# Sums with ones for the inverse roots at the gate and in the last product, and two of that product's four tiles in full width

## The chip, the cores and the metric

The kernel runs on one core of a Trainium2 chip. The metric is the device time of one execution in microseconds (us); lower is better. The profile is one execution recorded by the hardware profiler; its times count from the start of its span. The engines are called PE (TensorE's matmuls; PEld is its weight loads), DVE (VectorE), ACT (ScalarE), POOL (GpSimd) and SP (SyncE, which issues most DMAs).

## The reference

One decoder layer on 2048 tokens of 1024 channels, in float32: an RMSNorm, an input projection, two groups of heads (a gated linear recurrence and a sliding-window attention), an output projection, a second RMSNorm, a gated MLP, and a last RMSNorm. What matters here is the end of it:

```python
def rmsnorm(x, w, eps=EPS):
    inv = lax.rsqrt(jnp.mean(x * x, axis=-1, keepdims=True) + eps)
    return x * inv * w

h = h + mix @ w_out
v = rmsnorm(h, norm_ffn_w)
gate = causal_depthwise_conv(v @ w_gate, conv_w, conv_b)
h = h + (jax.nn.silu(gate) * (v @ w_up)) @ w_down
return rmsnorm(h, final_norm_w)
```

D_MODEL is 1024, the width of the MLP 2816. Each rmsnorm needs, for every token, the inverse root of the mean of 1024 squares.

## The kernel before, in words

**Layout.** Channels lie on the 128 partitions, tokens along the free dimension. The tokens go through the layer in two passes of 1024 (`hf` 0 and 1). A pass has the mixer stage, `out_proj` (line 785), `gate_up` (line 981) and `down` (line 1066); the end of `down` in pass 0 already loads and projects pass 1.

**Numbers in two parts.** A float32 operand of a large product is split into two float32r parts, the rounded value (`hi`, a cast on ACT, line 758) and the rest (`lo`, a subtraction on DVE, line 759); three matmuls (hi by hi, hi by lo, lo by hi) make the product. A matmul whose operands are plain float32, as the ones below, is carried out in two passes, and the profile shows two matmuls for it.

**Seven products.** `gate_up` and `down` multiply two-by-two blocks with seven products in place of eight (Strassen and Winograd's scheme). In `down` the products are called P1, P5, P6, P3, P7, P2 and P4 (the order in which they run); each runs over 11 blocks of 128 rows of `w_down`, taken in six pieces (five of two blocks, one of one) that SP loads and ACT and DVE split (`prep_piece`, line 1104). A product makes four output tiles (`d` 0 to 3) of 128 channels by 512 tokens, each in a PSUM bank of its own (`pdx` or `pdy`); `product` (line 1143) issues the three matmuls of each block, lines 1151 to 1153. After P2 the tokens' first half (`lo`, 512 of the pass's 1024) lacks only P4 in its upper four channel tiles; the second half (`hi`) was complete after P7.

**Sums of squares.** An object of `Stats` (line 241) keeps in `acc` the sum over the channel tiles of the squares (ACT squares, line 253; DVE adds, line 256), so that 128 partial sums per token are left, one in each partition. There are two ways from there to the inverse root:

- `inverse` (line 267) and `spread` (line 310): for each 128 tokens a matmul of `acc` as weights with one column of ones (line 276) puts the sum of a token into its own partition, as one column; `rsqrt` (line 170) works on 128x2 or 128x4 elements (DVE, three Newton steps from an integer guess; or, with `table`, ACT's Sqrt, a reciprocal and one step); the result is laid on a diagonal with the identity (line 284), and a matmul with ones (line 316) brings it to all partitions. In the last use, a series of 7 matmuls without use keeps PE at work meanwhile (`without_use`, line 281, `TAIL_WARM`).
- `everywhere` (line 296): a matmul of a 128x128 matrix of ones with `acc` (line 302) gives every partition the full sum of each token at once; ACT takes an approximate inverse root (line 304, `Abs_reciprocal_sqrt`) and its square (line 306), and DVE makes one Newton step at full width (lines 305, 307, 308). Its scratch tiles come from the ring `ut` of seven 128x512 tiles.

**At the gate.** In the first pair of channel tiles of `gate_up`, `everywhere` runs ahead of the product S4 (line 1012) over the pass's 1024 tokens, in two sums of 512. The roots scale the gate's tiles (line 1003) and later products; DVE and ACT split the next operands in the same stretch.

**P4 in the last pass.** The loop of `down` is left before P4 (line 1179), and P4 is written out (lines 1210 to 1234). The 512 tokens are taken in two halves of 256: for each half, for each of the four tiles, all 33 matmuls of 256 columns, then the addition to the residual (`add`, line 1137), its square and its sum (`st.add`), and the scaling by the final weight (`weigh`, line 1134). `inverse`, `spread` and `finish` of the 512 tokens that were complete before (`s2`) stand behind tiles of the first half, and those of the first 256 behind tiles of the second half. At the end come those of the last 256; there the square of the last tile isn't added to `acc` but summed by matmuls of its own. ACT loads its table for Sqrt ahead of that (line 1221).

**`finish`** (line 1241) multiplies the eight channel tiles by the root (line 1244, DVE) and issues a store after each (line 1245), on SP, or on ACT and SP in turn for the last 256.

**The order of the work.** The program text sets priorities; when the kernel is built, a scheduler with a timing model puts the instructions of each engine in a fixed order, by priority among those that it takes to be ready. `tc.issue_after(x)` puts what is traced within behind `x` on x's engine. Each engine then works in that order and waits on semaphores.

Of the kernel before, what the change touches and what calls it, by code (L numbers as in the profile page):

```python
# [8 lines left out]
F32 = mybir.dt.float32  # L9
F32R = mybir.dt.float32r  # L10
# [7 lines left out]
P = 128  # L18
# [22 lines left out]
UT = 7  # L41
# [12 lines left out]
def hymba_layer(ctx: ExitStack, tc: tile.TileContext, a: dict, out: bass.AP):  # L54
# [9 lines left out]
    wp = pool("w")  # L64
    hp = pool("h")
    sp = pool("small", bufs=2)
    sp.tile([P, 16], F32, name="pad", bufs=1)
    dp = pool("dram", space=bass.MemoryType.DRAM)
    mmp = pool("mm", bufs=4, space=PSUM)
    hgp = pool("hgp", bufs=2, space=PSUM)  # L70
# [3 lines left out]
    def ps(kind, name):  # L74
        return spaces[kind].tile([P, 512], F32, tag=kind, name=name)
# [164 lines left out]
    class Stats:  # L240
# [52 lines left out]
            nc.sync.dma_start(row, self.acc[0:1])  # L293
            nc.sync.dma_start(rs, row.rearrange("o (c t) -> (o t) c", t=P))

        def everywhere(self, part, kinds):

            n = self.acc.shape[-1]
            for b in range(n // 512):
                a = self.acc[:, b * 512:(b + 1) * 512]  # L300
                s = ps(kinds[b % 2], "psum")
                marks["psum"] = nc.tensor.matmul(s, ones, a, start=True, stop=True)
                y, t = part("y"), part("t")
                nc.scalar.activation(y, s, AF.Abs_reciprocal_sqrt, scale=1.0 / D, bias=eps)
                nc.vector.tensor_scalar(a, s, -0.5 / D, -0.5 * EPS, op0=ALU.mult, op1=ALU.add)
                nc.scalar.activation(t, y, AF.Square)
                nc.vector.tensor_tensor(t, t, a, op=ALU.mult)
                nc.vector.scalar_tensor_tensor(a, t, 1.5, y, op0=ALU.add, op1=ALU.mult)

        def spread(self, bank=None):  # L310

# [445 lines left out]
    def split_into(h, l, src, eng=None):  # L757
        return (nc.scalar.copy(h, src),  # L758
                (eng or nc.vector).tensor_tensor(l, src, h.bitcast(F32), op=ALU.subtract))  # L759
# [221 lines left out]
    def gate_up(hf, ops, hs, nxt, last, p):  # L981

        acts = {op: [dp.tile([P, n, 512], F32, name=f"act{hf}{op}{i}") for i, n in enumerate(PIECES)] for op in OPS}
        lo, hi = slice(0, 512), slice(512, HALF)
        invb = hs.acc

        def ring(name):
            return p.tile([P, 512], F32, tag="ut", name=name, bufs=UT)

        srcs = [w[2 * pr:2 * pr + 2] for pr in range(FT // 2) for w in (a["w_gate"], a["w_up"])]  # L990
        for pr in range(FT // 2):
            f0 = 2 * pr
            W, nxt = nxt, None

            ga = [p.tile([P, HALF + 64], F32, tag="ga", name="ga", bufs=2)[:, 0:2 + HALF] for _ in range(2)]

            def gate(i, j, x, y):
                dst = ga[i][:, 2 + j * 512:2 + (j + 1) * 512]
                iv = invb[:, j * 512:(j + 1) * 512]
                if y is not None:  # L1000
                    nc.vector.tensor_tensor(dst, x, y, op=ALU.add)
                    x = dst
                later.append(lambda: nc.vector.tensor_tensor(dst, x, iv, op=ALU.mult))
                if pr:
                    flush()

            def flush():
                while later:
                    later.pop(0)()

            later = []
            then = {"S4": lambda: hs.everywhere(ring, ("mm", "mm")), "A22": flush} if pr == 0 else {}
# [12 lines left out]
            for i in range(2):  # L1025
                ft, g = f0 + i, ga[i]
                nc.scalar.copy(g[:, 0:2], halo[:, ft])
# [36 lines left out]
        return acts  # L1064

    def down(hf, kept, acts, p):
# [4 lines left out]
        lo, hi = slice(0, 512), slice(512, HALF)  # L1071
        final = hf + 1 == NH
        NP = len(PIECES)
        def ring(name):
            return p.tile([P, 512], F32, tag="ut", name=name, bufs=UT)

        todo = [(name, w, t, j) for name, w, t in PRODUCTS for j in range(NP)]
        S = {}
# [53 lines left out]
        def weigh(d, bs):  # L1132
            t = hh[d][:, bs]
            return nc.scalar.activation(t, t, AF.Identity, scale=C.fnw[:, d:d + 1])

        def add(t, o):
            nc.vector.tensor_tensor(t, t, o, op=ALU.add)

        def done(st, d, bs):
            st.add(hh[d][:, bs])  # L1140
# [65 lines left out]
        if final:  # L1206
            for k in range(end + 3, len(todo)):
                ready[k] = prep_piece(k)

            steps = [(st, slice(i * 256, (i + 1) * 256)) for i, st in enumerate(s1.halves())]  # L1210
            for i, (st, bs) in enumerate(steps):
                for d in range(4):
                    for k in range(end, len(todo)):
                        product(k, bx[d][:, bs], d, bs)
                    t = hh[d + 4][:, bs]
                    add(t, bx[d][:, bs])
                    last = st.add(t, i == 1 and d == 3)
                    weighed = weigh(d + 4, bs)
                    if i and d == 0:
                        with tc.issue_after(weighed.ins):  # L1220
                            nc.scalar.activation(warm, ones[:, 0:1], AF.Sqrt)
                    if i == 0 and d == 0:
                        s2.inverse("o2")
                    elif i == 0 and d == 2:
                        s2.spread()
                        finish(hf, hh, s2, hi, [nc.sync])
                    elif i and d == 0:
                        steps[0][0].inverse("o")
                    elif i and d == 1:
                        inv = steps[0][0].spread(0)  # L1230
                    elif i and d == 2:
                        finish(hf, hh, steps[0][0], steps[0][1], [nc.sync], inv)
            steps[1][0].inverse("o", last)
            finish(hf, hh, steps[1][0], steps[1][1], [nc.scalar, nc.sync], steps[1][0].spread(1))
# [6 lines left out]
    def finish(hf, hh, st, bs, queues, inv=None):  # L1241
        for d in range(KT):
            t = hh[d][:, bs]
            nc.vector.tensor_tensor(t, t, st.acc if inv is None else inv, op=ALU.mult)
            queues[d % len(queues)].dma_start(out[d, :, hf * HALF + bs.start:hf * HALF + bs.stop], t)

    X = []
# [96 lines left out]
```

## Time and profile before

| what | us |
|---|---|
| median of 3 runs | 2122.56 |
| lowest and highest run | 2122.28 and 2124.97 |
| time of the profiled execution | 2122.11 |
| its span, first to last instruction | 2120.3 |

A line of the page's part 1 gives, per engine, the busy time, its share of the span and the number of instructions. A line of a timeline gives the start and the length (us), the engine, the line of the kernel, the operation, output and inputs by the program's names, the shapes, and in brackets the engine's idle time before it with the instruction that ended the wait. Rows named `x4` are merged from four instructions. A matmul's length runs from its start to the modelled end of its pipeline, so successive matmuls overlap; the distance between starts is the pace. A line of the chain of waits gives start, length, engine, output and line of one link.

### The profile page before, as it was taken

How to read it: one execution, taken by the hardware profiler on the slowest of the kernel's cores; microseconds unless marked ns; L12 is line 12 of the kernel's file. 1: busy time of each engine (PE TensorE's matmuls, PEld its weight loads, DVE VectorE, ACT ScalarE, POOL GpSimd, SP SyncE). 2: the span in 40 equal slices, each digit the busy share in tenths (PEclk: the TensorE clock that was granted, in tenths of full speed). 3: DMA queues.
4: the chain of work that ended last, by engine and by line, in shares of the span. 5: the costliest groups of instructions: out<-in, count | busy, mean ns of one | idle time of the engine just before them, and what ended most of it. 6: DMA issues, size and time to landing. Idle time of an engine off the chain costs nothing.

```text
span 2120.3 us, 29895 instructions
## 1 busy us (share of the span) xinstructions
PE 2108.2 (99%) x11584; PEld 1749.3 (83%) x11584; DVE 1624.7 (77%) x2374; ACT 1096.6 (52%) x1880; POOL 21.6 (1%) x52
## 2 busy tenths in 40 slices
PE   9999999999999999999999999999999999999998
PEld 7888888888888888888888888888888888888888
DVE  7457787898878878775863677868988787887766
ACT  6456675664444444435734476656544444443453
POOL 1000000000000000000000000000000000000000
PEclk9999999999999999999999999999999999999999
DMA  4111111423332325954731111213223223279643
GB/s 161 43 40 39 37 41 53 174 75 101 105 118 85 124 90 189 396 199 161 238 108 50 33 34 34 80 52 139 95 90 125 94 95 119 85 247 368 227 134 135
DMA packets 96475, 255.21 MB, mean 120 GB/s; under 512 B 17354, under 2 KB 19658, under 8 KB 96332
## 3 DMA queue, kind: packets, MB, share of 16 engines
q1 hardware_dynamic: 91076, 251.32, 34.6%
q10 hardware_dynamic: 5256, 1.98, 0.4%
q8 instruction: 91, 1.49, 0.3%
q14 instruction: 52, 0.43, 0.1%
HBM read 195.11 MB, written 57.16 MB: 119 GB/s over the span
## 4 chain that ended last, share of the span: by engine, by line
PE 82%; DVE 1%; DMA 1%; ACT 1%; issue 0%; DVEq 0%; ACTq 0%
PE pop L222 8%; PE X L933 7%; PE X L934 7%; PE X L935 7%; PE Y L933 4%; PE Y L934 4%; PE Y L935 4%; PE pdx L1151 3%; PE pdx L1153 3%; PE pdx L1152 3%; PE pdy L1151 3%; PE pdy L1153 3%; PE pdy L1152 3%; PE q L222 2%; PE g L222 2%; PE f L222 2%
## 5 line engine op out<-in xcount | busy, mean ns | idle before, releaser
L758 ACT CAST whi<-raw 128x1024 fp32r<-128x1024 f32 x88 | 92.7, 1053 | 102.9 <-PE X L934 61.1
L933 PE MATMUL X<-T,whi 128*128 128x512 f32 x352 | 137.0, 389 | 0.0
L934 PE MATMUL X<-T,whi 128*128 128x512 f32 x352 | 137.0, 389 | 0.0
L935 PE MATMUL X<-T,wlo 128*128 128x512 f32 x352 | 136.9, 389 | 0.0
L1032 DVE SCALAR_TENSOR_TENSOR y<-ga,cw,y 128x1024 f32<-128x1024 f32 x88 | 112.5, 1280 | 28.4 <-ACT y L1030 28.2
L940 ACT COPY u<-X 128x512 f32<-128x512 f32 x88 | 51.7, 587 | 124.1 <-PE X L935 124.1
L201 DVE TENSOR_TENSOR wlo<-raw,whi 128x1024 fp32r<-128x1024 f32 x57 | 69.4, 1222 | 59.4 <-ACT whi L200 59.0
L200 ACT CAST whi<-raw 128x1024 fp32r<-128x1024 f32 x57 | 59.4, 1048 | 95.7 <-PE hq L222 29.2
L759 DVE TENSOR_TENSOR wlo<-raw,whi 128x1024 fp32r<-128x1024 f32 x88 | 107.3, 1220 | 0.3 <-ACT whi L758 0.3
L222 PE MATMUL pop<-XH,whi 128*128 128x512 f32 x256 | 87.8, 393 | 0.0
L222 PE MATMUL pop<-XL,whi 128*128 128x512 f32 x256 | 87.4, 390 | 0.0
L222 PE MATMUL pop<-XH,wlo 128*128 128x512 f32 x256 | 87.0, 390 | 0.0
L759 DVE TENSOR_TENSOR xld<-raw,xhd 128x1024 fp32r<-128x1024 f32 x72 | 81.0, 1132 | 7.7 <-ACT xhd L758 7.5
L631 ACT COPY G<-QK 128x1024 f32<-128x1024 f32 x48 | 51.5, 1072 | 56.3 <-DVE QK L653 50.7
L758 ACT CAST xhd<-raw 128x1024 fp32r<-128x1024 f32 x72 | 69.5, 978 | 20.7 <-DMA raw<-act0B 5.8
L933 PEld LDWEIGHTS X<-T,whi 128*128 128x128 f32 x352 | 66.1, 188 | 14.1 <-ACT u L940 0.4
L934 PEld LDWEIGHTS X<-T,whi 128*128 128x128 f32 x352 | 66.1, 188 | 13.7
L935 PEld LDWEIGHTS X<-T,wlo 128*128 128x128 f32 x352 | 66.1, 188 | 13.7
L1151 PE MATMUL pdx<-xhd,hid 128*128 128x512 f32 x192 | 74.6, 392 | 0.9 <-ACT hid L758 0.6
L653 DVE TENSOR_TENSOR QK<-QK,f 128x1024 f32<-128x1024 f32 x56 | 68.5, 1223 | 8.3 <-ACT G L631 7.6
L1152 PE MATMUL pdx<-xld,hid 128*128 128x512 f32 x192 | 74.8, 389 | 0.0
L1153 PE MATMUL pdx<-xhd,lod 128*128 128x512 f32 x192 | 73.7, 389 | 0.0
(394 smaller groups left out, 6328.7 us busy)
## 6 DMA issues: line engine op xcount, KB each, us to landing
wr<-in_w_down SPq DMA_DIRECT2D x90, 512.0 KB, 4.7
raw<-in_w_gate SPq DMA_DIRECT2D x44, 512.0 KB, 3.6
raw<-in_w_up SPq DMA_DIRECT2D x44, 512.0 KB, 3.6
raw<-act0T SPq DMA_DIRECT2D x20, 512.0 KB, 5.5
raw<-act1T SPq DMA_DIRECT2D x20, 512.0 KB, 8.6
act0B<-y SPq DMA_DIRECT2D x33, 256.0 KB, 2.6
act1B<-y SPq DMA_DIRECT2D x33, 256.0 KB, 2.7
raw<-in_w_out SPq DMA_DIRECT2D x16, 512.0 KB, 5.6
```

Of the source, the lines that this page charges most:

```text
L201: nc.vector.tensor_tensor(lo, raw, hi.bitcast(F32), op=ALU.subtract)
L222: marks["unit"] = nc.tensor.matmul(o[b], w, x[:, bs], start=f, stop=l)
L653: done = nc.vector.tensor_tensor(own, own, Fv.rearrange("p b w -> p w b").unsqueeze(3).to_broadcast([P, 2, nb, m]), op=ALU.mult)
L758: return (nc.scalar.copy(h, src), (eng or nc.vector).tensor_tensor(l, src, h.bitcast(F32), op=ALU.subtract))
L759: (eng or nc.vector).tensor_tensor(l, src, h.bitcast(F32), op=ALU.subtract))
L933: nc.tensor.matmul(o, wh[:, ws], xh, start=i == 0 and not more, stop=False, skip_group_check=more)
L934: nc.tensor.matmul(o, wh[:, ws], xl, start=False, stop=False, skip_group_check=more)
L935: r = nc.tensor.matmul(o, wl[:, ws], xh, start=False, stop=i == 3, skip_group_check=more)
L1032: nc.vector.scalar_tensor_tensor(y, g[:, w:w + HALF], C.cw[:, ft, w:w + 1], y, op0=ALU.mult, op1=ALU.add)
L1151: nc.tensor.matmul(o, wh[:, i, c], ah[:, i, cols], start=f, stop=False, skip_group_check=more)
L1152: nc.tensor.matmul(o, wh[:, i, c], al[:, i, cols], start=False, stop=False, skip_group_check=more)
L1153: nc.tensor.matmul(o, wl[:, i, c], ah[:, i, cols], start=False, stop=l, skip_group_check=more)
```

## The change

Four edits.

1. `everywhere` can make its sum in two float32r parts (`two`): a cast and a subtraction split the 512 columns, and two matmuls with a float32r matrix of ones add them up. The gate uses this.
2. In the last pass P4 takes tiles 0 and 1 in full width (512 columns) and tiles 2 and 3 in two halves of 256. The order is: `everywhere` for the 512 tokens that are complete, tile 0, their `finish`, tile 1, the first halves of tiles 2 and 3, the first 256 tokens' inverse root, the second half of tile 2, half of the first 256 tokens' `finish`, the second half of tile 3, the other half of that `finish` behind the last addition, and then the last 256 tokens.
3. The inverse roots of the two lots of 256 tokens come from a new function `total`, which is `everywhere` for one lot of any width, with a second matmul for the last tile's squares. `inverse`, `spread` and the 7 matmuls without use are no longer called, nor is ACT's Sqrt table loaded.
4. A small padding tile grows from 16 to 48 elements per partition.

```diff
-        def everywhere(self, part, kinds):
+        def everywhere(self, part, kinds, two=False):
...
-                marks["psum"] = nc.tensor.matmul(s, ones, a, start=True, stop=True)
+                if two:
+                    hi, lo = part("hi", F32R), part("lo", F32R)
+                    split_into(hi, lo, a)
+                    nc.tensor.matmul(s, ones_r, hi, start=True, stop=False)
+                    nc.tensor.matmul(s, ones_r, lo, start=False, stop=True)
+                else:
+                    marks["psum"] = nc.tensor.matmul(s, ones, a, start=True, stop=True)
...
+        def total(self, part, kind, last=None):
+            a = self.acc
+            n = a.shape[-1]
+            s = ps(kind, "psum")[:, 0:n]
+            y, t = part("y")[:, 0:n], part("t")[:, 0:n]
+            more = last is not None
+            marks["psum"] = nc.tensor.matmul(s, ones, a, start=True, stop=not more, skip_group_check=more)
+            if more:
+                nc.tensor.matmul(s, ones, last, start=False, stop=True, skip_group_check=True)
+            nc.scalar.activation(y, s, AF.Abs_reciprocal_sqrt, scale=1.0 / D, bias=eps)
+            nc.vector.tensor_scalar(a, s, -0.5 / D, -0.5 * EPS, op0=ALU.mult, op1=ALU.add)
+            nc.scalar.activation(t, y, AF.Square)
+            nc.vector.tensor_tensor(t, t, a, op=ALU.mult)
+            nc.vector.scalar_tensor_tensor(a, t, 1.5, y, op0=ALU.add, op1=ALU.mult)
...
-            then = {"S4": lambda: hs.everywhere(ring, ("mm", "mm")), "A22": flush} if pr == 0 else {}
+            then = {"S4": lambda: hs.everywhere(ring, ("mm", "mm"), True), "A22": flush} if pr == 0 else {}
...
+            last = range(end, len(todo))
+
+            def column(d, cols, st, apart=False):
+                for k in last:
+                    product(k, bx[d][:, cols], d, cols)
+                t = hh[d + 4][:, cols]
+                added = add(t, bx[d][:, cols])
+                squares = st.add(t, apart)
+                weigh(d + 4, cols)
+                return added, squares
+
+            s2.everywhere(ring, aux)
+            column(0, lo, s1)
+            finish(hf, hh, s2, hi, [nc.sync])
+            column(1, lo, s1)
+            early, late = s1.halves()
+            c0, c1 = slice(0, 256), slice(256, 512)
+            for d in (2, 3):
+                column(d, c0, early)
+            early.total(ring, "hg")
+            column(2, c1, late)
+            finish(hf, hh, early, c0, [nc.sync], range(4))
+            added, squares = column(3, c1, late, True)
+            with tc.issue_after(added.ins):
+                finish(hf, hh, early, c0, [nc.sync], range(4, KT))
+            late.total(ring, "at", squares)
+            finish(hf, hh, late, c1, [nc.scalar, nc.sync])
```

What these lines replace is the loop over the two halves described above. `finish` gets an argument for the channel tiles that it takes, in place of the one for a root held in PSUM.

More of the change, by code (lines that the diff above doesn't have):

```diff
@@ L66, in hymba_layer @@
     sp = pool("small", bufs=2)
-    sp.tile([P, 16], F32, name="pad", bufs=1)
+    sp.tile([P, 48], F32, name="pad", bufs=1)
     dp = pool("dram", space=bass.MemoryType.DRAM)
@@ L985, in gate_up, with ring @@
         invb = hs.acc
-        def ring(name):
-            return p.tile([P, 512], F32, tag="ut", name=name, bufs=UT)
+        def ring(name, dt=F32):
+            return p.tile([P, 512], dt, tag="ut", name=name, bufs=UT)
         srcs = [w[2 * pr:2 * pr + 2] for pr in range(FT // 2) for w in (a["w_gate"], a["w_up"])]
@@ L1073, in down, with ring @@
         NP = len(PIECES)
-        def ring(name):
-            return p.tile([P, 512], F32, tag="ut", name=name, bufs=UT)
+        def ring(name, dt=F32):
+            return p.tile([P, 512], dt, tag="ut", name=name, bufs=UT)
         todo = [(name, w, t, j) for name, w, t in PRODUCTS for j in range(NP)]
@@ L1136, in add @@
         def add(t, o):
-            nc.vector.tensor_tensor(t, t, o, op=ALU.add)
+            return nc.vector.tensor_tensor(t, t, o, op=ALU.add)
         def done(st, d, bs):
@@ L1208, in down @@
                 ready[k] = prep_piece(k)
[L1210 to L1232, printed above, removed]
@@ L1233, in down @@
-            steps[1][0].inverse("o", last)
-            finish(hf, hh, steps[1][0], steps[1][1], [nc.scalar, nc.sync], steps[1][0].spread(1))
+            last = range(end, len(todo))
[7 more added lines that the diff above has]
+                return added, squares
@@ L1239, in down, with finish @@
         return X, kv, xs.acc, xs.rs, f0
-    def finish(hf, hh, st, bs, queues, inv=None):
-        for d in range(KT):
+    def finish(hf, hh, st, bs, queues, some=range(KT)):
+        for d in some:
             t = hh[d][:, bs]
-            nc.vector.tensor_tensor(t, t, st.acc if inv is None else inv, op=ALU.mult)
+            nc.vector.tensor_tensor(t, t, st.acc, op=ALU.mult)
             queues[d % len(queues)].dma_start(out[d, :, hf * HALF + bs.start:hf * HALF + bs.stop], t)
```

## The prediction

> **What bounds the kernel now.** I read the page first, then the busy time by stretches of the span, then the chain of waits at the end, then the timeline of each engine around the two places that the change touches.
>
> ```profile
> span 2120.3 us, 29895 instructions
> PE 2108.2 (99%) x11584; PEld 1749.3 (83%) x11584; DVE 1624.7 (77%) x2374; ACT 1096.6 (52%) x1880; POOL 21.6 (1%) x52
> ```
> ```profile
> 40.00:2110.00 2070.00, 2067.68 (x11405) 1717.07 (x11404) 1589.50 (x2312) 1066.96 (x1843) 14.55 (x27) 1.00 0.35 118
> ```
>
> The first column of the second fence is the stretch, then its length, then busy time of PE, PEld, DVE, ACT and POOL, the granted clock, the DMA share and GB/s. Between 40 us and 2110 us TensorE (PE) idles 2.3 us of 2070 at full clock. So a microsecond of PE work that goes anywhere in there comes off the end, unless something else is late when PE arrives. After 2110 the kernel is a chain:
>
> ```profile
> 2110.25 0.43 DVE h L1137
> 2110.71 0.42 ACT fsq L262
> 2111.18 0.62 PE pst L276 x4
> ...
> 2113.57 0.71 PE pinv L316 x2
> 2114.31 0.42 DVE h L1244
> ```
>
> Each row is start, length, engine, output and line. Call T0 = 2110.25 the last addition of the last product. The first final multiplication comes 4.06 us later, and from there to the end of the span (multiplications, stores, their landing) it is 5.99 us. The change can thus pay in two ways: PE time before T0, and links of this chain.
>
> **Part 1, the last product: two tiles in full width.** PE's pace is the distance between starts, not the length of a row. I take two rows of one line, 48 steps apart in both cases (16 rounds of L1151, L1152, L1153):
>
> ```profile
> 2060.12 0.39 PE L1151 MATMUL pdy<-xhd,gad 128*128 128x512 f32 x1
> ...
> 2071.00 0.39 PE L1151 MATMUL pdy<-xhd,hid 128*128 128x512 f32 x1
> 2100.28 0.28 PE L1151 MATMUL pdx<-xhd,xh2d 128*128 128x256 f32 x1
> ...
> 2106.03 0.28 PE L1151 MATMUL pdx<-xhd,xh2d 128*128 128x256 f32 x1
> ```
>
> 512 columns: 10.88 / 48 = 226.7 ns. 256 columns: 5.75 / 48 = 119.8 ns. Two halves cost 239.6, so a full-width step saves 12.9 ns. A tile has 11 blocks of weights with three matmuls each, 33 steps; two tiles give 66 x 12.9 = 0.85 us of PE.
>
> The page "TensorE: Matmul & The Clock Gate" of the Trainium skill (Part 1, on the 56 ns gap) has a warm matmul start N / 2.4 GHz plus about 2.5 ns after the one before, so a full-width step would save only those 2.5 ns, 0.17 us in all, and the whole sum below would be 3.6 us instead of 4.2. This trace disagrees: its fixed part, from the two paces above (2 x 119.8 - 226.7), is 12.9 ns. I go by the rows.
>
> **Part 2, the last product: sums with ones.** Gone are the matmuls of one column each (line 276), eight for the second half of the columns, four for the first quarter; the four plus four of the last quarter lie after T0.
>
> ```profile
> 2077.55 0.28 PE L1153 MATMUL pdx<-xhd,xl2d 128*128 128x256 f32 x1
> 2077.67 0.95 PE L276 MATMUL pst<-ones,invb 128*128 128x1 f32 x8
> ...
> 2078.69 0.28 PE L1152 MATMUL pdx<-xld,xh2d 128*128 128x256 f32 x1
> 2099.59 0.28 PE L1152 MATMUL pdx<-xld,xh2d 128*128 128x256 f32 x1
> ```
>
> Without the eight, L1151 and L1152 would have started at 2077.67 and 2077.79; L1152 starts at 2078.69: 0.90 us. At 2099.59 an L1152 runs, L1153 and the next L1151 would follow at 2099.71 and 2099.83, and that L1151 stands above at 2100.28: 0.45 us for the four. Together 1.35 us of PE go.
>
> The spreading matmuls (line 316) go too, but a sum with ones of the same width, in the same two float32 passes, takes the place of each:
>
> ```profile
> 2088.83 0.86 PE pinv L316 x2
> ...
> 2106.55 0.43 PE pinv L316 x2
> ```
>
> A 512-column sum at the gate costs 0.86 by part 4; so 0.86 for 0.86 and 0.43 for 0.43, nothing won or lost on PE. What else comes lies on ACT and DVE: per sum a root, a square and three passes over the width, while some eleven short DVE operations, an expansion with the identity and an ACT copy go. Before T0 this is hidden behind columns of 4 to 7.5 us of PE. The table load that stood at 2098.93 now comes at the start of the last product; rival 3 prices the cover it needs.
>
> **Part 3, the chain after T0.** The trace has no such chain at 256 columns, but one at 512, ending a half of the first pass:
>
> ```profile
> 1072.18 1.02 PE L302 MATMUL psum<-sums,ones 128*128 128x512 f32 x2
> 1073.24 0.69 ACT L304 ACTIVATE y<-psum,warm 128x512 f32<-128x512 f32 x1 [3.87 <-PE psum L302]
> 1073.96 0.63 ACT L306 ACTIVATE t<-y 128x512 f32<-128x512 f32 x1
> 1073.96 0.69 DVE L305 TENSOR_SCALAR sums<-psum 128x512 f32<-128x512 f32 x1 [3.33 <-ACT y L304]
> 1074.76 0.69 DVE L307 TENSOR_TENSOR t<-t,sums 128x512 f32<-128x512 f32 x1
> 1075.48 0.69 DVE L308 SCALAR_TENSOR_TENSOR sums<-t,y 128x512 f32<-128x512 f32 x1
> ```
>
> L305 starts only when the root has ended, so the links follow one another. A square takes 0.63 at 512 and 0.42 at 256 (L306, L262): 0.21 less on ACT. DVE takes 0.69 at 512 and 0.43 at 256 (L1137). From T0: addition and square as before, the sum starts at 0.93; like the 256-column spreading matmul it needs 0.74 to its reader (2113.57 to 2114.31); root 0.48 + 0.03; square or L305 with the wait behind them 0.53; L307 and L308 0.45 each. First multiplication at T0 + 3.61 against T0 + 4.06: 0.45 us gained. The other sum of the pair is ready early and runs in PE's idle time before it. With ACT and DVE at their 512-column lengths it would be T0 + 4.6, a loss of 0.6; had I overrated each of the five links by a tenth of a microsecond, a gain of 0.9.
>
> The warming matmuls go: at half clock the sum would take 0.71 us more. The clock row against it:
>
> ```profile
> 2118.00:2118.50 0.50, 0.00 (x0) 0.00 (x0) 0.00 (x0) 0.00 (x0) 0.00 (x0) 0.69 0.97 332
> ```
>
> It falls only here, almost 4 us after PE's last work (2114.28); before the new sum PE rests less than one. I take nothing.
>
> Four multiplications of the third quarter now stand on DVE between the last addition and the last chain: 4 x 0.33 from T0 + 0.45, done at T0 + 1.8, before L305 needs DVE at about T0 + 2.2. Free, with 0.4 us of cover. Their stores on SP: rival 4.
>
> **Part 4, the gate, twice.** Two 512-column sums in float32:
>
> ```profile
> 436.23 0.39 PE L934 MATMUL Y<-B,S 128*128 128x512 f32 x1
> 436.46 1.88 PE L302 MATMUL psum<-invb,ones 128*128 128x512 f32 x4
> ...
> 438.40 0.39 PE L933 MATMUL Y<-B,S 128*128 128x512 f32 x1
> ```
>
> At the pace of 0.227 this L933 would have started at 436.69: 1.71 us. Four float32r matmuls take 4 x 0.227 = 0.91. PE saves 0.80, in both passes 1.60 us. Each pass pays with two casts on ACT (0.6 each) and two subtractions on DVE (0.6 each at back-to-back pace), ahead of the sum.
>
> ```profile
> 430.00:455.00 25.00, 25.00 (x109) 19.99 (x108) 24.79 (x38) 15.17 (x25) 0.00 (x0) 1.00 0.16 47
> 435.98 0.19 ACT L1027 COPY ga<-halo 128x2 f32<-128x2 f32 x1 [1.91 <-PE X L934]
> 448.21 1.22 DVE L759 TENSOR_TENSOR Sl<-S,Sh 128x1024 fp32r<-128x1024 f32 x1
> ...
> 452.27 0.39 PE L935 MATMUL X<-T,Sl 128*128 128x512 f32 x1
> ```
>
> ACT idles 1.91 us just there: the casts are free. DVE has no room (24.79 of 25 us), so all that it delivers afterwards is 1.2 us later. The tightest delivery that I found is Sl: done at 449.43, used at 452.27, 2.8 us of cover. The delay takes 1.2, PE's earlier arrival 0.8: 0.8 is left. I count the full 1.60.
>
> **Sum.** 0.85 + 1.35 + 0.45 + 1.60 = 4.25, given as 4.2: the profiled span goes to 2116.1, its own time from 2122.11 to 2117.9. The median of the runs, 2122.56, lies 0.45 above that execution; on it I predict 2118.4. 0.2% is 4.24 us, and about the least that measurements of this kernel can tell from no change: the forecast stands on that line.
>
> **Rivals.**
> 1. The gate gives it back. If DVE, at 99% there, is what PE waits for, each pass costs 1.2 - 0.8 = 0.4 instead of saving 0.8: gain 1.8, 2120.8. For it: 24.79 of 25. Against: the 2.8 us before Sl.
> 2. The pace does not follow the width: if full-width steps of this product ran at twice 119.8, part 1 is nothing: 2119.2. Against: the 226.7 measured in the product just before, with the same loop. The rule of the Trainium skill quoted in part 1 ("TensorE: Matmul & The Clock Gate", Part 1) would end close to it, at 2119.0.
> 3. PE waits for the last weights; this ends slower than before.
>
> ```profile
> 2085.22 0.68 DVE L759 TENSOR_TENSOR xl2d<-wr,xh2d 128x512 fp32r<-128x512 f32 x1
> 2098.93 1.28 ACT L1221 ACT_TABLE_LOAD   x1
> 2075.00:2086.00 11.00, 11.00 (x91) 10.85 (x90) 9.44 (x20) 8.11 (x12) 0.00 (x0) 1.00 0.43 163
> ```
>
> The last low part is ready at 2085.90. A table load, a root and a square ahead of the casts (1.28 + 0.69 + 0.63) make it 2088.5. The product starts near 2075.8 (2110.1 less 264 steps of 0.1198 and the 2.64 of part 2's matmuls); the 18 steps of the first three pieces of one tile, after the sum, end at 2080.7. If PE then stood until 2088.5 and ran the last 3 steps, tile one ends at 2089.2, not 2084.1: 5.1 us lost, 2123.5. It decides from 4.2 us of waiting; slower by over 0.2% needs 8.5. Against: in the last row PE never idles although pieces arrive till 2085.9, so steps of other tiles fill in; those ready (18 of each of two full and two half tiles, 12.5 us) reach to 2089.1.
> 4. SP is late with the last stores. The four moved stores are issued by T0 + 2.2, the last quarter's begin on SP at T0 + 4.4. One issue in the trace took far longer than the usual 0.33:
>
> ```profile
> 2109.14 2.13 SPq L1245 DMA_DIRECT2D out<-h  x1
> ```
>
> Among the four, it fits in the gap of 2.2; among the last ones it costs up to 2.1: 2120.5.
>
> **How the numbers follow.** Forecast 0.62 (2117.6 to 2119.2: the ends of part 3, and some tenths of waits), rival 1 0.15, rival 2 0.05, rival 3 0.06, rival 4 0.08; 0.04 for a gain up to 1 us larger. Over half of the forecast's chance lies beyond the line: 0.36, with the 0.04 a chance of 0.40 for faster by over 0.2%. Slower by over 0.2% is the far end of rival 3 with mishaps at the gate: 0.05. The rest, 0.55, is within. The range 2117.2 to 2121.2 holds all but rival 3 and the edges.
>
> **What would show it.** Right: steps of 128x512 in P4 at 227 ns; last addition 2.2 us nearer to the start of the product; first multiplication about 3.6 us after it; four gate matmuls in 0.9 us without PE idle behind them until 470. Wrong: PE rows with idle time released by DVE wlo or Sl after the gate, or by xl2d in the last product; SP issues over 1 us after the last addition; T0 + 4 or more.

## The result and the profile after

| | kernel before | kernel after |
|---|---|---|
| median of 22 runs each, us | 2123.23 | 2119.65 |
| lowest and highest | 2122.05 and 2125.39 | 2118.4 and 2123.98 |
| profiled execution, its span | 2122.11, 2120.3 | 2121.16, 2119.4 |

The ratio is 0.9984 (95% interval 0.9978 to 0.9990): 3.6 us faster, between 2.1 and 4.7. The forecast was 4.2 us and a median of 2118.4. The profiled execution after lies 1.5 us above its median and that of before 1.1 below its own, so the two spans differ by less than the medians do; what follows compares stretches, not spans.

The page after, and the busy times by stretches (40 to 2110 us, then the stretch around the first gate):

```profile
span 2119.4 us, 29666 instructions
PE 2102.8 (99%) x11486; PEld 1741.5 (82%) x11486; DVE 1626.4 (77%) x2353; ACT 1097.6 (52%) x1883; POOL 22.8 (1%) x52
```
```profile
40.00:2110.00 2070.00, 2064.93 (x11328) 1712.04 (x11327) 1589.69 (x2290) 1067.35 (x1845) 14.57 (x27) 1.00 0.35 118
430.00:455.00 25.00, 25.00 (x111) 20.39 (x110) 23.58 (x35) 15.95 (x26) 0.00 (x0) 1.00 0.21 64
```

PE idles 5.07 us of the 2070 where it idled 2.32: it was given less work, and part of that came out as waiting. Most of the waits that are new stand at three places: 0.93 us at K (below), 0.72 at P1's weights in the first pass (at 851.31) and 0.51 ahead of P1 in the second. The last row shows DVE 23.58 us busy of 25 where it had 24.79, although it was given two subtractions more.

The last product begins at 2077.70. Two rows 33 steps apart of full width, then two of half width, on the timeline of PE:

```profile
2086.22 0.39 PE L1174 MATMUL pdx<-xld,xh2d 128*128 128x512 f32 x1
...
2093.70 0.28 PE L1174 MATMUL pdx<-xld,xh2d 128*128 128x256 f32 x1
...
2098.73 0.28 PE L1174 MATMUL pdx<-xld,xh2d 128*128 128x256 f32 x1
...
2099.09 0.28 PE L1174 MATMUL pdx<-xld,xh2d 128*128 128x256 f32 x1
```

From 2086.22 to 2093.70 are 33 steps: 226.7 ns each. From 2098.73 to 2099.09 are three: 120 ns. Then the chain of waits at the end:

```profile
2110.03 0.43 DVE h L1159
2110.48 0.42 ACT fsq L262
2110.95 0.71 PE psum L325 x2
2111.69 0.48 ACT y L326
2112.20 0.44 DVE invb L327
2112.72 0.44 DVE t L329
2113.18 0.43 DVE invb L330
2113.64 0.43 DVE h L1268
```

T0, the last addition, is 2110.03; the first final multiplication follows 3.61 us later (4.06 before). The eight links are the eight that the prediction listed, each within 0.03 us of its length.

Five stretches carry the comparison. G is the first matmul into X of a pass's `gate_up` to the first matmul of P1 (425.44 to 837.59 in the first pass after), less a wait right ahead of P1. K is PE's wait in the second pass's first projection (`kv`, line 222), at the end of the first pass. P is the first matmul of P4 to T0; C is T0 to the first of the last multiplications; E is from there to the end of the span.

| kernel | median us | ratio to before (95%) | G, pass 1 / 2 | K | P | C | E |
|---|---|---|---|---|---|---|---|
| before | 2123.23 | | 412.48 / 412.48 | 0.16 | 34.49 | 4.06 | 5.98 |
| after | 2119.65 | 0.9984 (0.9978 to 0.9990) | 412.15 / 412.19 | 1.09 | 32.33 | 3.61 | 5.78 |
| e9_again (after, again) | 2119.74 | 0.9985 (0.9976 to 0.9993) | 412.16 / 412.17 | 0.96 | 32.33 | 3.61 | 5.79 |
| e1_no_gate | 2120.11 | 0.9983 (0.9973 to 0.9992) | 412.48 / 412.48 | 0.18 | 32.33 | 3.62 | 5.78 |
| e2_gate_only | 2123.30 | 0.9995 (0.9986 to 1.0004) | 412.14 / 412.15 | 0.32 | 34.47 | 4.06 | 5.96 |
| e3_halves | 2123.27 | 0.9999 (0.9990 to 1.0008) | 412.17 / 412.17 | 1.22 | 35.68 | 3.60 | 6.37 |
| e4_hi_only | 2120.23 | 0.9981 (0.9972 to 0.9990) | 411.32 / 411.31 | 1.49 | 32.33 | 3.61 | 5.79 |
| e5_lo_pool | 2119.36 | 0.9981 (0.9973 to 0.9990) | 411.84 / 411.79 | 0.21 | 32.33 | 3.61 | 6.32 |
| e6_ring8 | 2122.26 | 0.9994 (0.9985 to 1.0003) | 413.41 / 413.41 | 0.95 | 32.33 | 3.61 | 5.81 |
| e7_all_two | 2126.24 | 1.0012 (1.0003 to 1.0021) | 412.10 / 412.09 | | 31.94 | 3.61 | 6.29 |
| e8_stores_first | 2121.35 | 0.9991 (0.9982 to 1.0000) | 412.14 / 412.11 | 2.29 | 33.24 | 3.61 | 5.79 |
| e10_pool_p4 | 2119.05 | 0.9982 (0.9973 to 0.9991) | 411.81 / 411.81 | 0.21 | 31.97 | 3.61 | 6.07 |
| e11_full_width | 2123.05 | 0.9999 (0.9990 to 1.0008) | 412.13 / 412.13 | 0.74 | 31.02 | 5.53 | 8.34 |
| e12_roots_only | 2122.75 | 1.0000 (0.9991 to 1.0009) | 412.11 / 412.09 | 1.20 | 34.88 | 3.61 | 6.33 |

(The blank in e7's row: its first pass ends otherwise, told below.) Each ratio is to runs of the kernel before from the same batch, so rows are compared by ratio rather than by median. G, P and C repeat to some hundredths wherever the code of the stretch is the same; whole times are known to about 2 us. So the stretches decide, and the whole times say only whether a stretch's gain got through.

After against before, by stretches: P 2.16 less, C 0.45 less, E 0.20 less, G 0.33 and 0.29 less, K 0.93 more: 2.5 us. P and C are as forecast; G gave 0.62 where 1.60 was forecast, and a wait of 0.9 came at a place that the prediction did not name. (The profiled spans differ by 0.9 us only: the two waits at P1, and 0.35 more of one at line 514, account for nearly all of the rest.)

### The profile page after: what moved, and what is told of

Its sections match the earlier page's. It is cut to its first block, busy times and chain, and to the rows that moved or that the text cites. A ratio compares the mean times of both kernels' runs of the same rounds, so it can differ in the third digit from the quotient of the medians.

```text
span 2119.4 us, 29666 instructions
## 1 busy us (share of the span) xinstructions
PE 2102.8 (99%) x11486; PEld 1741.5 (82%) x11486; DVE 1626.4 (77%) x2353; ACT 1097.6 (52%) x1883; POOL 22.8 (1%) x52
## 3 DMA queue, kind: packets, MB, share of 16 engines
q8 instruction: 90, 1.47, 0.3%
## 4 chain that ended last, share of the span: by engine, by line
PE 81%; ACT 2%; DVE 1%; DMA 1%; issue 0%; DVEq 0%; ACTq 0%
PE X L955 8%; PE X L956 8%; PE X L957 8%; PE pop L222 7%; PE Y L957 4%; PE Y L956 4%; PE Y L955 4%; PE pdx L1173 3%; PE pdx L1174 3%; PE pdx L1175 3%; PE pdy L1173 3%; PE pdy L1174 3%; PE pdy L1175 3%; PE q L222 2%; PE hq L222 2%; PE f L222 2%
```

## The experiments

**The gate: alone, and left out.** The theory was that the gate is worth little and the last product carries the gain; the rival was that the gate's 1.6 us are there.

```
e1_no_gate, against after:
-            then = {"S4": lambda: hs.everywhere(ring, ("mm", "mm"), True), "A22": flush} if pr == 0 else {}
+            then = {"S4": lambda: hs.everywhere(ring, ("mm", "mm")), "A22": flush} if pr == 0 else {}
e2_gate_only, against before: everywhere() and ring() as after, and
+            then = {"S4": lambda: hs.everywhere(ring, ("mm", "mm"), True), "A22": flush} if pr == 0 else {}
```

> The changed kernel with the gate's sums back in float32 (edit 1 undone), the last product as changed. Read on the trace by stretches: from the gate's first matmul to the first of P1, without the wait right ahead of P1, the kernel before takes 412.5 us (pass 1) and 412.6 (pass 2), the changed one 412.2 and 412.3. Theory A (the prediction: the gate's float32r sums save 0.8 a pass): 412.9 to 413.1 here, and 1.6 us slower than the changed kernel. Theory B (half of it is lost to PE steps that come late behind the sums): back at 412.5 and 412.6, and about 0.6 slower. From the first matmul of P4 to the last addition 32.3 us in both theories, as in the changed kernel (34.5 before), and 3.6 from there to the first final multiplication.

> The kernel before with the gate's sums in two float32r parts alone (edit 1 alone). Theory A: 1.6 us faster than before, the gate's stretch to P1 0.8 shorter in each pass. Theory B: about 0.6 faster, the stretch 0.3 shorter (412.2 and 412.3), with a step of PE that comes 0.1 to 0.4 late some 20 us after the sums. P4 and the end as before: 34.5 and 4.06 us.

Without the gate's parts the kernel stays at 0.9983, and with them alone it is at 0.9995, with 1 inside the interval: the gate is worth nothing that the whole time can tell. G moves with the gate alone, by 0.33 us a pass, whatever the last product does; theory B, half of the gate's gain lost, has the size right.

**What the gate's gain is lost to.** Three kernels: the rounded part alone, so that neither the second matmul nor DVE's subtraction is there; the subtraction on GpSimd; and a scratch ring of eight tiles, in case the parts' tiles hold up the ring.

```
e4_hi_only:
-                    hi, lo = part("hi", F32R), part("lo", F32R)
-                    split_into(hi, lo, a)
-                    nc.tensor.matmul(s, ones_r, hi, start=True, stop=False)
-                    nc.tensor.matmul(s, ones_r, lo, start=False, stop=True)
+                    hi = part("hi", F32R)
+                    nc.scalar.copy(hi, a)
+                    nc.tensor.matmul(s, ones_r, hi, start=True, stop=True)
e5_lo_pool:
-                    split_into(hi, lo, a)
+                    split_into(hi, lo, a, nc.gpsimd)
e6_ring8:
-UT = 7
+UT = 8
```

> The changed kernel with the high part alone in the gate's sums: the two subtractions on DVE and the two matmuls of the low parts are left out, so the roots there are a little off. PE has 2 x 0.227 us less a pass. If DVE's extra 1.2 us is what costs the gate half of its gain (theory B1), the late steps vanish and the stretch gets shorter by 0.45 + 0.3 or more: 411.4 or less. If the order of the instructions or the scratch tiles cost it (theory B2), it gets shorter by 0.45 alone, 411.7, and late steps remain.

> The changed kernel with the gate's two subtractions a pass on GpSimd, which is idle there, in place of DVE. Scratch tiles, casts and matmuls stay. The kernel with the high parts alone had a stretch of 411.32 us against 412.15: 0.83 shorter, of which 0.45 are matmuls that it leaves out; it also uses two scratch tiles less and no DVE. Theory B1 (DVE's 1.2 us cost the rest): the stretch is about 411.8 here, the late steps behind the sums gone, if GpSimd is no slower than some 2 us for a subtraction. Theory B3 (the seven scratch tiles hold the second sum up): the stretch stays at 412.15 or gets longer.

> The changed kernel with eight scratch tiles in the ring that the gate's casts, roots and copies share, in place of seven. Theory B1 (DVE's work is what costs): the stretch from the gate to P1 stays at 412.15. Theory B3 (slots): the second sum's cast no longer stands 7 us behind the first, and the stretch falls to 411.8 or less.

e4 shortens G by a further 0.83 us: two matmuls less are 0.45, so 0.38 goes with the subtractions. e5 keeps both matmuls and gains 0.33 over after: the loss goes with the subtractions' place on DVE. That is the number of theory B1, but not by its mechanism, DVE's time, as the rows below show. The timelines of POOL and of DVE in e5:

```profile
437.42 2.47 POOL L781 TENSOR_TENSOR lo<-invb,hi 128x512 fp32r<-128x512 f32 x1 [145.82 <-ACT ga L1049]
444.18 1.29 POOL L781 TENSOR_TENSOR lo<-invb,hi 128x512 fp32r<-128x512 f32 x1 [4.29 <-ACT hi L780]
```
```profile
439.25 1.19 DVE L781 TENSOR_TENSOR T<-v,T 128x512 fp32r<-128x512 f32 x1
...
444.50 1.52 DVE L917 TENSOR_TENSOR raw<-raw,S 128x512 f32<-128x512 f32 x1
```

GpSimd takes 2.47 and 1.29 us for what DVE does in 0.68, and the sums still have time. But DVE is not relieved: the step that is on DVE when GpSimd ends takes 1.19 and 1.52 in place of 0.68, in all four gate passes of e5 and e10, 1.35 us together where 1.2 were taken away, and DVE's busy time from 430 to 462 is 31.13 us in e5 and 30.34 after. The Trainium skill says in "SBUF — State Buffer" (Who interferes with whom) that a two-input step of DVE with both inputs in SBUF contends with GpSimd's reads of it; these rows agree. So G is shorter in e5 without DVE having less to do.

Where PE loses the time can be read from the distances of starts. Both kernels take 1816 steps in G, nearly all of 0.227 us. What the steps over 0.24 us take beyond that adds up to 0.34 us after and 0.05 in e5, close to the 0.31 by which G differs. Of the 0.34, 0.27 stand in two neighbouring steps 36 us into the stretch. After, PE and then ACT there:

```profile
461.03 0.39 PE L957 MATMUL X<-T,Sl 128*128 128x512 f32 x1
461.25 0.39 PE L955 MATMUL X<-B,whi 128*128 128x512 f32 x1
461.48 0.39 PE L956 MATMUL X<-B,whi 128*128 128x512 f32 x1
461.71 0.39 PE L957 MATMUL X<-B,wlo 128*128 128x512 f32 x1
462.10 0.50 PE L955 MATMUL X<-T,whi 128*128 128x512 f32 x1
462.43 0.39 PE L956 MATMUL X<-T,whi 128*128 128x512 f32 x1
```
```profile
461.45 0.59 ACT L962 COPY u<-X 128x512 f32<-128x512 f32 x1 [0.84 <-PE X L957]
```

The step from 461.71 takes 0.39 and the next 0.33 in place of 0.227. The matmul at 462.10 begins 0.06 after the end of ACT's copy out of the tile X that was finished at 461.42; the trace's view of its line names that copy (line 962) as what it waited for, and only three matmuls (from 461.25) stand between. In e5 the same place on PE reads:

```profile
460.22 0.39 PE L957 MATMUL X<-T,Sl 128*128 128x512 f32 x1
460.44 0.39 PE L956 MATMUL Z<-B,whi 128*128 128x512 f32 x1
...
461.35 0.39 PE L957 MATMUL Z<-B,wlo 128*128 128x512 f32 x1
461.58 0.39 PE L955 MATMUL X<-T,whi 128*128 128x512 f32 x1
```

Here five matmuls of Z, 1.1 us, stand behind the finished X, and no step is long. So the place of the subtraction moved the order on PE as the scheduler fixed it, and that order uncovered the copy. Runs of the same output on PE show it too: the eight kernels whose G is 412.1 to 412.2 (after, e2, e3, e7, e8, e9, e11, e12) have twelve of Z and then thirty-six of X in a row there, and the same two long steps; e5 and e10 have Z in two fives between the X, e4 a ten of Z, and none of the three has a long step there. That the order does it, and not DVE's time, is supported by this and by DVE's busy time in e5, but not shown: no run changed the order alone.

e6 gains nothing from the longer ring: G is 1.26 longer than after. The timeline of PE shows most of it:

```profile
445.68 0.50 PE L305 MATMUL psum<-hi,ones_r 128*128 128x512 f32 x1 [0.99 <-ACT hi L780]
```

PE now waits for the second sum's cast: another order again (ACT's table load at 442.48 follows the first sum, where after has it at 439.21, ahead of it). As the order changed too, the ring alone stays untested.

**The same two parts at five more sums.** If each were worth its PE time, five would save 2 us.

```
e7_all_two (xs is 1024 wide and makes two sums; s2 stands twice, once in each pass):
-            s2.everywhere(ring, aux)
+            s2.everywhere(ring, aux, True)
-  3: lambda: s1.everywhere(ring, aux), 7: lambda: (xs.everywhere(ring, aux), xs.column())
+  3: lambda: s1.everywhere(ring, aux, True), 7: lambda: (xs.everywhere(ring, aux, True), xs.column())
```

> The changed kernel with the other 512-column sums outside the first load in two float32r parts too (in pass 1's end three kinds, four sums; and the sum ahead of P4 in pass 2): five sums, 0.86 down to 0.45 each on PE. Theory A (a float32r sum saves its 0.4 wherever PE is the bound): 2.0 us faster than the changed kernel. Theory B (what ACT and DVE do ahead of it gives half back): 0.5 to 1.0 faster. Slower is possible where the sum waits for its low part: PE would then show waits for DVE at the sums.

By the ratios 2.6 us slower than before and 6 behind the changed kernel. P4's own sum pays as worked out (P 31.94 against 32.33), but at the end of the first pass PE then stands still:

```profile
1096.37 0.80 PE L222 MATMUL hq<-XH,whi 128*128 128x512 f32 x1 [5.96 <-DVE vT L468]
```

The matmul waits for the multiplication by the root (line 468), and the root is late. After, the two sums of `xs` follow each other on PE (1080.39 and 1080.84). In e7 the second's cast begins on ACT at 1083.73, behind the first's root and square, and its last matmul comes at 1090.01, 8 us behind the first's (1082.04). A cast and a subtraction take 1.3 us by their rows; the rest of the delay is their place in the fixed order. One wait of 5.96 eats all.

**The width of the tiles.** P contains the width, the sums and the order. e3 and e12 undo the width alone, in two orders; e11 takes it to all four tiles.

```
e3_halves, in place of full-width tiles 0 and 1:      e12_roots_only:
 column(0, c0, early)                                  column(0, c0, early)
 finish(hf, hh, s2, hi, [nc.sync])                     finish(hf, hh, s2, hi, [nc.sync])
 column(1, c0, early)                                  for d in (1, 2, 3): column(d, c0, early)
 column(0, c1, late)                                   early.total(ring, "hg")
 column(1, c1, late)                                   for d in (0, 1, 2): column(d, c1, late)
 (tiles 2 and 3 as after)                              (from here as after)
e11_full_width:
 finish(hf, hh, s2, hi, [nc.sync])     (behind tile 0, as after)
 for d in (1, 2): column(d, lo, s1)
 added, squares = column(3, lo, s1, True)
 s1.total(ring, "at", squares)
 finish(hf, hh, s1, lo, [nc.scalar, nc.sync])
```

> The changed kernel with tiles 0 and 1 of P4 in halves too, taken as 0 and 1 first halves, 0 and 1 second halves, and then as in the changed kernel. From P4's first matmul to the last addition the changed kernel takes 32.33 us. Theory A (the pace row: 12.9 ns for each of 66 steps saved): 33.2 here and 0.85 us slower. Rival (the pace follows the product, not the width, or the Trainium skill's 2.5 ns a step): 32.3 to 32.5. The gate's stretch 412.15 as in the changed kernel, the end as there.

> As the changed kernel with its sums with ones, but all four tiles of the last product in halves, in the order of the kernel before: the width is the only thing undone, and no addition has to wait for the multiplications of another lot in between. By the pace of the rows (12.9 ns a step, 66 steps) first matmul to last addition takes 32.33 + 0.85 = 33.2 us; by a fixed part of 2.5 ns a matmul it takes 32.5. T0 + 3.61 and the end stay. The whole is 0.85 (or 0.2) slower than the changed kernel. A wait of PE in this stretch as in the kernel with tiles 0 and 1 halved (35.7) would have to come from the weights, not from the order.

> As the changed kernel, but all four tiles of the last product in full width; its columns 0 to 511 then have one sum at the very end and eight final multiplications of 512 columns. PE before the last addition falls by 2 x 33 x 12.9 ns = 0.85 us and by the early sum, 0.43: first matmul to last addition 31.05 instead of 32.33, with the last addition itself 0.25 longer. The chain grows with the width: about T0 + 5.2 (0.69 for 0.43 three times on DVE, 0.63 and 0.69 for 0.42 and 0.48 on ACT, a sum of 0.43 more) instead of 3.61, and from there to the end eight multiplications of 0.6 instead of 0.33 and twice the bytes stored, 2.2 us or more on top of 5.8. The whole is about 2.5 to 3 us slower than the changed kernel. Rival: the stores overlap so well that the end is not longer than by 1 us; then the whole is about 1.3 slower.

Both e3 and e12 miss: 35.68 and 34.88 for 33.2. The width costs about what was said; a wait comes on top. DVE and then PE in e12:

```profile
2088.78 4.91 DVE L1268 TENSOR_TENSOR h<-h,invb 128x512 f32<-128x512 f32 x8
2093.61 1.41 DVE L1159 TENSOR_TENSOR h<-h,pdx 128x256 f32<-128x256 f32 x4
```
```profile
2092.61 0.28 PE L1175 MATMUL pdx<-xhd,xl2d 128*128 128x256 f32 x1
2094.08 0.39 PE L1173 MATMUL pdx<-xhd,xh2d 128*128 128x256 f32 x1 [1.19 <-DVE h L1159]
```

The eight multiplications of `finish` hold DVE for 4.9 us, four additions stand behind them, and PE needs the bank that the first of them frees. Two steps of P are long in e12, 1.47 us from 2092.61 and 0.33 from 2086.43, in place of 0.12 each: 1.56 us. 34.88 - 1.56 = 33.3, 1.0 above the 32.33 with two full tiles (0.85 by the rows). e3 has the same wait, and its last addition stands behind four multiplications besides, 0.5 us late. e12's expectation was wrong in saying that no addition waits there: I had left `finish` where the changed kernel has it, behind the first tile, where the kernel before has it later. In full width a tile lasts 7.5 us and 4.9 us of `finish` pass within it: after, the same eight multiplications run from 2091.14 and PE never waits. So with this place of `finish` the full width is worth 2.55 us, of which about 1.6 are the wait.

e11 takes the other 0.85 and the early sum away before T0 (31.02, expected 31.05), and pays at the end (C 5.53, expected 5.2; E 8.34, expected 8.0 or more). The chain of waits of e11 from T0:

```profile
2108.12 0.70 DVE h L1159
...
2109.52 1.14 PE psum L325 x2
...
2110.69 0.70 ACT y L326
...
2113.65 0.69 DVE h L1260
```

Each link is the 512-column one. By the ratios, 0.9999 against 0.9984, it ends 3.2 us behind the changed kernel. Two full tiles and two in halves are a middle between PE's time before T0 and the chain after it.

**The four multiplications behind the last addition.**

```
e8_stores_first:
-            finish(hf, hh, early, c0, [nc.sync], range(4))
+            finish(hf, hh, early, c0, [nc.sync])
             added, squares = column(3, c1, late, True)
-            with tc.issue_after(added.ins):
-                finish(hf, hh, early, c0, [nc.sync], range(4, KT))
```

> As the changed kernel, but all eight multiplications and stores of the quarter before the last go ahead of tile 3's last 33 steps; none is held back behind the last addition. My theory has the four held back for free: then the stretch from the first matmul of the last product to the last addition stays 32.33 us, the first final multiplication stays at T0 + 3.61, the time from it to the end stays 5.8 (6.3 where the landing happens to be late), and the whole stays within 0.2 us of the changed kernel. Rival A, that the four cost the chain something on DVE or on SP: T0 + 3.3 to 3.5 or an end 0.2 to 0.5 nearer. Rival B, that they are needed where they are, since eight multiplications (8 x 0.33 = 2.6 us) ahead of the last additions hold DVE: last addition up to 0.5 us later, the whole 0.5 slower.

My theory misses. DVE and then PE in e8:

```profile
2107.76 2.77 DVE L1266 TENSOR_TENSOR h<-h,invb 128x256 f32<-128x256 f32 x8
2110.45 0.41 DVE L1159 TENSOR_TENSOR h<-h,pdx 128x256 f32<-128x256 f32 x1
```
```profile
2109.35 0.59 PE L323 MATMUL psum<-invb,ones 128*128 128x256 f32 x2
2111.37 0.70 PE L325 MATMUL psum<-fsq,ones 128*128 128x256 f32 x2 [1.43 <-ACT fsq L262]
```

PE is done with the product at 2109.5 and the last addition comes only at 2110.45, behind all eight. P is 0.91 longer: rival B, at twice its size. Held back, the four are free; ahead, they cost 0.9.

**The changed kernel again, and a candidate.** e10 joins what gained in its own stretch: the subtractions on GpSimd, and two parts at P4's sum.

```
e9_again: no edit
e10_pool_p4:
-                    split_into(hi, lo, a)
+                    split_into(hi, lo, a, nc.gpsimd)
-            s2.everywhere(ring, aux)
+            s2.everywhere(ring, aux, True)     (line 1243, in P4)
```

> The changed kernel once more, for the spread of what lies outside the touched places. Its first profile had 2.4 us more of PE waits between 40 and 2110 us than the profile of before, most of it at P5's weights of pass 1 (1.0 against 0.28) and at the first projection of pass 2 (1.1 against 0.16). Theory C (these differ from run to run): they are near 0.3 and 0.2 here, and the span near 2117.5. Theory D (they belong to the changed order): they are at 1.0 and 1.1 again. The gate's stretch 412.15, P4 32.33, the last chain 3.61 in both.

> As the changed kernel, with the two subtractions of each gate pass on GpSimd instead of DVE, and the first sum of the last product in two float32r parts as well. If what keeps the gate from paying is DVE's 1.2 us, both gate stretches take 411.8 instead of 412.16; two parts save 0.4 us in the last product: first matmul to last addition 31.94 instead of 32.33. Together 1.1 us less than the changed kernel. If the wait of about 1 us at the first projection of the second pass also comes from DVE's subtractions, it falls to 0.2 to 0.3 and the gain is 1.9. Rival: GpSimd's subtraction is slow beside a busy DVE and the part in the last product comes late for its sum: stretch 32.3 or more, gain 0.7 or less.

e9 repeats all stretches within 0.15 us. Theory D holds for K (0.96 again), theory C for the weights (0.28, as before; the traces show them to be P1's, `pdx`, not P5's). PE idles 3.28 us between 40 and 2108.5 in e9. In e10, G is 411.81 in both passes, P 31.97 and K 0.21, as expected, 2.0 us together by the stretches; E is 0.29 longer than after in this trace. The whole, 0.9982 (0.9973 to 0.9991), can't be told from the changed kernel's 0.9984, nor can e5's 0.9981. They beat the kernel before; whether they beat the changed one stays open.

**The wait K.** It stands in the first projection of the second pass; PE before, then PE and ACT after:

```profile
1058.42 0.74 PE L222 MATMUL kv<-XH,wlo 128*128 128x512 f32 x2 [0.16 <-DVE wlo L201]
```
```profile
1059.86 0.73 PE L222 MATMUL kv<-XH,wlo 128*128 128x512 f32 x2 [1.09 <-DVE wlo L201]
```
```profile
1049.85 1.16 ACT L236 ACTIVATE XH<-x,nmw 128x1024 fp32r<-128x1024 f32 x1 [1.79 <-DMA x<-in_xT]
```

It is 0.16 to 0.32 in before, e1, e2, e5 and e10, and 0.74 to 2.29 in the others. The order of DVE, ACT and PE there is the same in all these kernels. DVE's delivery follows a chain in which ACT waits for loads of `x` (line 236): at 1049.85 it had waited 1.79 us for one, in e1 1.71 at 1048.42. From the start of that step on ACT to the matmul above it is 10.0 us before and after, 10.1 in e1, and 9.3 to 10.1 in all thirteen kernels; PE is ready for the matmul 9.8 us behind that step before, 9.9 in e1 and 8.9 after. So the end of the wait goes with the load of `x` far more closely than with PE's arrival, and K is mostly what PE is early by against that load; these are thirteen traces side by side, and no run moved the load alone. That GpSimd's subtraction cures it, as e5 and e10 suggest, doesn't hold: e4, with no subtraction at all, waits 1.49. Nor is the change's code all of it: e3, e8, e11 and e12 differ from after only behind this place, and K is 0.74 to 2.29 in them. What sets the load's time against PE is open.

## Why the prediction was right, point by point

- **Bound.** Right for the last product: P is 2.16 us shorter, with no wait of PE in it, and PE stayed at full clock between 40 and 2110. The condition "unless something else is late" counted elsewhere: PE's idle time grew by 2.75 us in the profiled execution.
- **Part 1, full width, 0.85, and part 2, sums with ones, 1.35.** Right as a sum: 2.16 for 2.20. The pace is 226.7 and 120 ns; e12 puts the width at 1.0, with the long steps taken out, which leaves 1.2 for the sums. The two single sizes are thus known to about 0.15 only. The rule of the Trainium skill that was weighed there ("TensorE: Matmul & The Clock Gate", Part 1) would have made the width 0.17; the measurement decides against it for these matmuls. Rival 2 falls with it.
- **Part 3, the chain.** T0 + 3.61 was said and 3.61 measured, without the warming matmuls. The four multiplications cost nothing where they stand; e8 shows that they have to stand there. E was 0.2 shorter than before, but 5.78 to 6.37 over kernels with the same end, so I count no gain from it; why it falls on either side is open.
- **Part 4, the gate.** This failed: "I count the full 1.60". It gave 0.62, and the step that went wrong is the one before it, in which DVE's 1.2 us were set against the 2.8 us of cover of Sl alone. Sl was not late. With the subtractions on DVE the order on PE is another, and 0.27 of each pass's loss of about 0.5 stands at one X bank whose copy had lost its cover. With the subtractions on GpSimd a pass saves 0.66 of the 0.80. Rival 1 (DVE as the bound, a loss of 0.4 a pass) is wrong as well: G got shorter, and DVE's busy share fell.
- **The rest of what is missing** is K, 0.9 us, a wait that I had not priced. In the traces it outweighs the gate: after saves 0.6 us in G against e1, which is without the gate, and waits 0.9 longer in K. That fits the two whole times, which can't be told apart, but they are too coarse to show it.
- **Rival 3, the last weights.** Did not occur, since the table load stands behind the last cast (2086.87, the last cast before it) and PE waited for no piece. **Rival 4, SP's last stores.** Did not occur: all twelve stores that SP issues at the end take 0.33 to 0.41 us each, and the eight early ones are issued by 2112.65, ahead of the next on SP at 2114.43.
- **The total.** 4.25 forecast; by stretches 2.5, by medians 3.6 with an interval of 2.1 to 4.7, which holds both. What held of the sum are parts 1 to 3, 2.65 of it and 2.61 measured, read off rows of the same operations, the links at 256 columns scaled from 512. The stretches add up to little over half of the forecast; that the medians lie nearer to it no run explains, and so much of the nearness is luck.

## What to carry to other kernels

Price a PE edit by distances of starts of the same shape in the trace, and a chain link by the row of the same width: the last product as a whole and the chain came out within 0.05 us here. Where an edit adds work to an engine that feeds PE, looking at the one tightest delivery is not enough: it can also change the fixed order, so look for places where a bank is reused soon after its copy, and try the added step on an idle engine too. Long runs of elementwise work ahead of an addition that frees a bank cost PE directly; a wider tile, or issuing half of the run behind the last addition, hides them.

## What the runs showed of the hardware that was not expected

- A 128x512 subtraction took GpSimd 2.47, 1.29 and 1.83 us in three places where DVE's rows show 0.68. In the gate's two places a step on DVE beside it was 0.5 and 0.84 us longer: moving it there took nothing off DVE.
- The table load took 1.28 us, and the root stood 0.01 behind its end; placed behind the last cast of the last product it cost PE nothing:

```profile
2086.87 1.28 ACT L310 ACT_TABLE_LOAD   x1
2088.16 0.69 ACT L310 ACTIVATE y<-psum,warm 128x512 f32<-128x512 f32 x1
```

- In the eleven traces that end with the same eight multiplications and stores (the changed kernel's), the time from the first of them to the end of the span lay at 5.8 us in six traces and at 6.1 to 6.4 in five. No run looked for the reason.
